# Program order for the loads of the transposed weight sections of a two-layer hybrid encoder

## The chip, the cores and the metric

The kernel runs on one core of one Trainium2 chip. The metric is the device time of one execution in microseconds (us); of several runs the median counts. A profile is one more execution, taken by the hardware profiler; its times are counted from the start of its span. The engines are called PE (TensorE, matmuls), PEld (its weight loads), DVE (VectorE), ACT (ScalarE), POOL (GpSimd) and SP (SyncE, which here issues every DMA).

## The reference

Two layers, each `x <- x + W_out(concat[A(h) * silu(g_A), B(h) * silu(g_B)])` with `h = RMSNorm(x)`, on 2048 tokens of width 1024, and a last RMSNorm. All inputs and the output are float32.

```python
def hybrid_layer(x, norm_gain, w_in, w_out, rel_bias, cos, sin):
    hn = rms_norm(x, norm_gain)
    proj = hn @ w_in                      # 1024 x 4096
    aq, ak, av, ag, rq, rk, rv, rg = jnp.split(proj, cuts, axis=-1)
    ya = chunked_rel_attention(aq, ak, av, rel_bias)   # 8 heads x 64, own chunk + 8 before
    yr = chunkwise_retention(rq, rk, rv, cos, sin)     # 4 heads x 128, recurrent over chunks
    y = jnp.concatenate([ya * silu(ag), yr * silu(rg)], axis=-1)
    return x + y @ w_out
```

A is a softmax attention with a learned bias by distance; B is a retention with decay, rotary phases and an RMS norm for each head.

## The kernel before, in words

Every float32 operand of a dense product is split into an upper and a lower half in float16, and three products of halves are summed, so a 128x512 result of depth 1024 takes 24 matmuls.

**Tiling.** A layer's heads are worked in four groups s = 0 to 3 (two attention heads and one retention head each), and a group's 2048 tokens in four blocks n = 0 to 3 of 512. A stage is named (layer, group, block). In each stage `dense_T` (L620) computes q, k of the attention and q, k of the retention, transposed (results `dT`, matmuls at L746), and `dense_V` (L753) the values and gates (`dV`, L766). One stage later `attention` (L792) and `retention` (L881) work on the block, between the dense matmuls.

**Rounds.** `run` (L1158) draws the work in rounds: eight dense matmuls (a third of a result), then what is due of the delayed steps (`tick`), a list's entry, a step of the attention, the entry's second half, and one or more steps of the background work (`pull`). dense_T and dense_V have twelve rounds each. The attention of a block has 24 rounds: every third issues the scores of one unit (128 tokens of one head, eight units in a block), and the product with v (`o`, L836 and L837) of a unit is issued some six rounds later. Between them lie DVE (bias and maximum, L818), ACT (exponential and upper half, L821 and L823), POOL (lower half, L824) and SP: one round after the scores, L826 transposes the probabilities of the unit by DMA (`pT<-pq`, up to 128x1280 elements of float16).

**Weight sections.** A group's weights come in sections of 1024x128 floats (512 KB): four for dense_T (`stT`, class `Sections`, L359) and four for dense_V (`stV`, `prep_V`, L434). `load_sec` (L295, its DMA at L300) puts a section into a slot of the pool `w4`, which has three. ACT squares it (L317) with a row sum, DVE casts the sum (`mbT`, L324), PE adds over the partitions (`ms`, L331), DVE makes a power of two of it (L144 and the following lines), and ACT and DVE split the section into its halves (L338, L341). Then the slot is free. `prep_T` (L402) does this for the next group's dense_T in 25 steps of background work, started in the round 0 of (l, s, 1): step 1 loads section 0, step 2 section 1, step 3 squares section 0, step 8 loads section 2, step 9 squares section 1, step 14 loads section 3, steps 15 and 21 square sections 2 and 3. The first round takes two steps, the later ones one.

**Group 1 of layer 0** is prepared by a list written out by hand (L1476 and the following lines). It has one entry for each of the first 96 rounds, from round 0 = the first of dense_V of (0,0,0), to which `weight_steps` (L1208) adds the names: `Tin0` to `Tin3` load the dense_T sections, `Tsq0` to `Tsq3` square them, `Uin0` and so on do the same for dense_V. In the same rounds the names `xin`, `xsq`, `xhi`, `xlo`, `xdma` load, normalise, split and transpose the last blocks of x, the tokens' tiles 12 to 15 going through the same slots of `w4`, and `v` is a step of the rotary tables.

**The order of the work.** PE, ACT, DVE and POOL execute in the order in which the program is traced. SP's queue does not: the compiler's scheduler fills it by its own estimate of when each DMA's inputs and slot are there, so a load whose slot is free can stand far ahead of its place in the program. Slots of a pool go to tiles in the order in which these are made. `in_turn` (L589) is the exception: it calls `tc.keep_in_program_order`, by which an instruction may not be queued ahead of the SP instruction traced just before it. Already in turn are the stores of y (L852, L926), the copies of q (L654), the rotary tables (L629, L630), a group's first bias tile (L576) and section 2 of each dense_V (L434). Each queue's instructions are issued in order, and SP waits at the head of its queue.

Of the kernel before, what the change touches and what calls it, by code (L numbers as in the profile page):

```python
# [18 lines left out]
P = 128  # L19
# [8 lines left out]
def hybrid_trunk(ctx: ExitStack, tc: tile.TileContext, x, pos, gain, gcol, w_in, w_out, rel, fgain,  # L28
# [6 lines left out]
    NS = SEQ // 512  # L35
# [259 lines left out]
    def load_sec(src, nm, halves=False, turn=False):  # L295

        v = src.rearrange("(k p) c -> p k c", p=P)
        if not halves:
            st = w4.tile([P, KT, P], F32, tag="w4", name=f"st{nm}")
            i = sp.dma_start(st, v)  # L300
            if turn:
                in_turn(i)
            return [(st, 0, KT)]
        h = KT // 2
        st = [b2.tile([P, 3 - i, 512], F16, tag=("rot2", "rot3")[i], name=f"st{nm}_{i}") for i in range(2)]
        st = [t_[:, 0:2].rearrange("p a c -> p (a c)").bitcast(F32).rearrange("p (k c) -> p k c", c=P) for t_ in st]
        for i in range(2):
            sp.dma_start(st[i], v[:, i * h:(i + 1) * h, :])
        return [(st[i], i * h, (i + 1) * h) for i in range(2)]
# [49 lines left out]
    class Sections:  # L359
# [15 lines left out]

        def load(self, j):
            o = TSEC[j] * 512 + self.s * P
            self.sts.append(load_sec(w_in[self.l, :, o:o + P], f"{self.nm}{j}", self.halves))

        def squares(self, j):  # L380
            nm = f"{self.nm}{j}"
# [177 lines left out]
    def bias_scratch(l, s):  # L559
        for hh in range(2):  # L560
            h = 2 * s + hh
            d = dp.tile([P * RELW], F32, tag=f"toep{h % 4}", name=f"toep{l}_{h}")
            i = sp.dma_start(d.rearrange("(p w) -> p w", w=RELW),
                             rel_d[l * 8 + h:l * 8 + h + 1, 1:RELW + 1].to_broadcast([P, RELW]))
            if (l, s) != (0, 0):
                tc.keep_in_program_order(i)
            toep[l, h] = d
        yield

    def bias_tiles(l, s, g):  # L570

        g.bias = []
        for hh in range(2):
            h = 2 * s + hh
            bt = b3.tile([P, 640], F32, tag="bias", name=f"bias{l}_{h}")
            i = sp.dma_start(bt, toep[l, h][127:127 + P * (RELW - 1)].rearrange("(p w) -> p w", w=RELW - 1)[:, 0:640])  # L576
            if hh == 0:
                in_turn(i)
            yield
            pool.memset(bt[64:128, 0:64], NEG)  # L580
            pool.memset(bt[0:64, 576:640], NEG)
            act.activation(bt, bt, AF.Copy, scale=g.ci[:, 0:1])
            g.bias.append(bt)
            yield
# [4 lines left out]
    def in_turn(i):  # L589

        if not ring.get("free"):
            return
        tc.keep_in_program_order(i)
# [9 lines left out]
    def later(k, fn):  # L603
        deferred.append([k, fn])
# [529 lines left out]
    def push(gen, steps):  # L1134
        bg.append([gen, steps])
# [11 lines left out]
    def drain(gen):  # L1147
        for _ in gen:
            pass
# [3 lines left out]
    def grp(l, s):  # L1153
        if (l, s) not in groups:
            groups[l, s] = Grp()
        return groups[l, s]
# [184 lines left out]
    def go_on(*gens):  # L1341
        for g_ in gens:
            next(g_, None)
# [123 lines left out]
    def do(names):  # L1467
        for nm in names.split():
# [24 lines left out]
    LAYER = [("", "yl0 yl1"), ("ys1", ""), ("", "xl0"), ("ys0", "yc0"), ("", "yh0"), ("", "yc1"), ("", ""),  # L1493
# [31 lines left out]
    for l in range(DEPTH):  # L1525
        gO = [Grp(), Grp()]
        go = Grp()
        for s in range(NSW):
            g = grp(l, s)
            for n in range(NS):  # L1530
                first = (l, s, n) == (0, 0, 0)
                if not first:
                    st = St()
                    states[l, s, n] = st
                    dT = dense_T(l, s, n, g, st)
                else:
                    st = st0
                if n == 0 and not first:
                    bs, bt = bias_scratch(l, s), bias_tiles(l, s, g)
                    later(3, lambda bs=bs: next(bs))  # L1540
                    for k in (7, 11, 17, 21):
                        later(k, lambda bt=bt: next(bt))
                if (l, s) == (0, 0) and 0 < n < NS - 1:
                    pairs = [xs0[0], w4.tile([P, D], F32, tag="w4", name="rows8") if n == 1 else xs0[1]]
                    pairs = [(w_[:, 0:D], w_[:, D:2 * D]) for w_ in (r_.bitcast(F16) for r_ in pairs)]
                    norm_steps(range(4 * n + 4, 4 * n + 8), late[0:4] if n == 1 else None, pairs)
                    if n == 2:
                        t3 = tables((3,), [xs0[3][:, i * 256:(i + 1) * 256] for i in range(4)])
                        steps["v"] = lambda: go_on(t3)
                if (l, s, n) == (0, 1, 2):  # L1550
                    for l_ in range(1, DEPTH):
                        gr = gain_scale(l_)
                        later(2, lambda gr=gr: next(gr))
                        later(10, lambda gr=gr: next(gr))
                        later(18, lambda gr=gr: next(gr))
                if (l, s, n) == (0, 0, NS - 1):
                    weight_steps()
                elif n == 1 and (l, s) != (0, 0):
                    if s + 1 < NSW:
                        push(prep_T(l, s + 1, grp(l, s + 1)), 25)  # L1560
                    else:
                        push(prep_O(l, gO[0], go), 9)
                if n == NS - 1 and s == 1 and l + 1 < DEPTH:
                    gain_load(l + 1)
                if n == 2 and 0 < s < 3:
                    push(prep_Omax(l, go, 4 * s - 4, 4 * s), 13 if s == 1 else 16)
                last = n == NS - 1 and s == NSW - 1
                if last:
                    us = []
                    sections = layer_steps(l, go, gO, us)  # L1570
                    ring["listed"] = iter(LAYER if l + 1 < DEPTH else LAST)
                if not first:
                    run(dT, att, 12 if last else 10 if n == 0 else 18 if (l, s, n) == (0, 0, NS - 1) else 22 if (l, s) == (0, 0) else 24)
                if n == NS - 1 and (l, s) != (0, 0):
                    if s + 1 < NSW:
                        push(prep_V(l, s + 1, grp(l, s + 1)), 23)
                run(dense_V(l, s, n, g, st), att, 24 if n == NS - 1 and s < NSW - 1 else 12)
                if first:
                    sp_order.__exit__(None, None, None)
                    ring["free"] = True  # L1580
                if att[0] is not None:
                    drain(att[0])
                att = [attention(l, s, n, g, st, states.get((l, s, n - 1)))]
        pull(1000)
        if l + 1 == DEPTH:
            ring["fg"] = b3.tile([P, D], F32, tag="wh", name="fg")
            sp.dma_start(ring["fg"], fgain.to_broadcast([P, D]))
        wT = sections() if l + 1 < DEPTH else None
        wo = wout(l, go, gO, us, wT)

        def rounds_of(k):
            run((next(wo) for _ in range(k)), att, k)

        rounds_of(6 * NT - 6)
        run(wo, att, 15)
# [60 lines left out]
```

## Time and profile before

| | |
|---|---|
| three runs | 2003.07, 2003.18, 2006.47 us |
| median | 2003.18 us |
| the profiled execution's own time | 2003.99 us |
| its span, first to last instruction | 2002.2 us |
| PE busy | 1976.9 us |
| DVE, ACT, POOL busy | 1231.6, 1155.0, 700.2 us |
| DMA engines busy with queue 1 | 68.1% of 16 engines' span |
| loads of `stT` at L300 | 27, of which 24 belong to groups 1 to 3 |

A row of the timeline reads: start, duration, engine and line, operation, out<-in, and in brackets how long the engine sat idle before it and what ended that. SPq is SP's queue; the duration of its row is that of the issue, not of the transfer. A row of waits reads: who waited, for whom, the sum in us, how often, the longest. In rows of groups the three figures of a duration are minimum, median and maximum in ns, and the last line of such a view gives the time from a DMA's issue to its landing in us. A busy time of PE has the modelled ends of its matmuls in it, which overlap.

### The profile page before, as it was taken

The page shows a single profiled execution, that of the slowest core. Times are in us where ns is not written, and L with a number is a line of the kernel's source. Part 1 is how long each engine was busy: PE and PEld are TensorE (multiplying, and loading weights), DVE is VectorE, ACT ScalarE, POOL GpSimd, SP SyncE. Part 2 cuts the span into 40 slices and gives each one's busy share as a digit, 9 for nine tenths or more (in the row PEclk, how much of TensorE's full clock was granted, in tenths as well). Part 3 has the DMA queues.
Part 4 walks back from the last instruction along what each step waited for, and adds up shares of the span by engine and source line. Part 5 has one row for each costly group of instructions (what it writes and reads, how often), then busy time and mean ns, then how long its engine had stood idle before and what let it go on. Part 6 is the DMA issues. An engine that isn't in the chain of part 4 may idle for free.

```text
span 2002.2 us, 36754 instructions
## 1 busy us (share of the span) xinstructions
PE 1976.9 (99%) x12894; PEld 1041.2 (52%) x12894; DVE 1231.6 (62%) x3664; ACT 1155.0 (58%) x2522; POOL 700.2 (35%) x701
## 2 busy tenths in 40 slices
PE   7999999999999999999999999999999999999998
PEld 5455555555555555554444555555555555555544
DVE  8787756665656655677544556555655565557544
ACT  8667756565656645656345556565656565456432
POOL 1444333434444334420013444344343443343100
PEclk9999999999999999999999999999999999999999
DMA  8899756576556655899974457564756575558864
GB/s 253 194 189 191 168 118 135 134 156 136 126 133 143 143 121 116 197 235 275 241 175 99 102 114 169 120 148 104 173 120 148 106 179 125 122 121 194 234 200 137
DMA packets 651706, 315.05 MB, mean 157 GB/s; under 512 B 465248, under 2 KB 608096, under 8 KB 651520
## 3 DMA queue, kind: packets, MB, share of 16 engines
q1 hardware_dynamic: 651520, 312.70, 68.1%
q8 instruction: 101, 1.65, 0.4%
q14 instruction: 85, 0.70, 0.1%
HBM read 123.26 MB, written 41.98 MB: 83 GB/s over the span
## 4 chain that ended last, share of the span: by engine, by line
PE 92%; DMA 3%; ACT 1%; SPq 1%; DVE 1%; issue 1%; POOL 1%; POOLq 0%; ACTq 0%; DVEq 0%
PE dV L766 31%; PE dT L746 30%; PE dO L1114 16%; PE r L871 4%; PE o L836 3%; PE S L814 3%; PE S L815 3%; PE o L837 2%; DMA pT<-pq 1%; DMA hTh<-in_x_dram 0%; SPq L1400 0%; DMA stT<-in_w_in_dram 0%; DMA yly<-hTh 0%; DMA hTl<-in_x_dram 0%; SPq L543 0%
## 5 line engine op out<-in xcount | busy, mean ns | idle before, releaser
L824 POOL TENSOR_TENSOR pq<-sc,pq 128x640 f16<-128x640 f32 (+4 forms) x256 | 322.5, 1260 | 957.4 <-ACT pq L823 482.5
L821 ACT ACTIVATE sc<-sc,mq,cT 128x640 f32<-128x640 f32 (+4 forms) x256 | 218.4, 853 | 403.9 <-DVE mq L820 291.9
L766 PE MATMUL dV<-whV,hTh 128*128 128x512 f16 x1024 | 351.5, 379 | 0.0
L766 PE MATMUL dV<-wlV,hTh 128*128 128x512 f16 x1024 | 351.5, 379 | 0.0
L766 PE MATMUL dV<-whV,hTl 128*128 128x512 f16 x1024 | 351.5, 379 | 0.0
L746 PE MATMUL dT<-hTh,whT 128*128 128x512 f16 x1008 | 346.6, 379 | 0.7 <-PE dV L766 0.7
L746 PE MATMUL dT<-hTh,wlT 128*128 128x512 f16 x1008 | 346.6, 379 | 0.0
L746 PE MATMUL dT<-hTl,whT 128*128 128x512 f16 x1008 | 346.6, 379 | 0.0
L766 PEld LDWEIGHTS <-hTh 128*128 128x128 f16 x2048 | 196.0, 98 | 211.6 <-DVE gt L784 0.4
L746 PEld LDWEIGHTS <-whT 128*128 128x128 f16 x2016 | 192.1, 98 | 206.0 <-issue 1.1
L818 DVE CUSTOM_DVE_ANT_0 sc<-S,bias 128x640 f32<-128x640 f32 (+4 forms) x256 | 188.5, 736 | 140.7 <-PE S L815 139.9
L1114 PE MATMUL dO<-whO,yhy 128*128 128x512 f16 x504 | 191.0, 379 | 1.2 <-DMA yhy<-hTh 1.2
L1114 PE MATMUL dO<-whO,yly 128*128 128x512 f16 x504 | 191.0, 379 | 0.2 <-DMA yly<-hTh 0.2
L1114 PE MATMUL dO<-wlO,yhy 128*128 128x512 f16 x504 | 191.0, 379 | 0.0
L823 ACT ACTIVATE pq<-sc 128x640 f16<-128x640 f32 (+4 forms) x256 | 171.5, 670 | 8.1
L1114 PEld LDWEIGHTS <-yhy 128*128 128x128 f16 x1008 | 98.0, 98 | 114.5 <-DMA yhy<-hTh 1.4
L766 PEld LDWEIGHTS <-hTl 128*128 128x128 f16 x1024 | 99.0, 98 | 109.8
L746 PEld LDWEIGHTS <-wlT 128*128 128x128 f16 x1008 | 97.4, 98 | 108.3 <-DVE wlT L1437 0.3
L814 PE MATMUL S<-k,q 128*128 128x128 f16 (+3 forms) x592 | 142.4, 267 | 0.0
L836 PE MATMUL o<-v,pT 128*128 128x129 f16 x1120 | 132.4, 221 | 3.1 <-DMA pT<-pq 3.0
L815 PE MATMUL S<-k,q 128*128 128x128 f16 (+3 forms) x592 | 129.3, 266 | 0.0
L837 PE MATMUL o<-v,pT 128*128 128x65 f16 x1120 | 125.7, 193 | 0.0
(359 smaller groups left out, 3245.0 us busy)
## 6 DMA issues: line engine op xcount, KB each, us to landing
q<-qq SPq DMA_DIRECT2D x128, 128.0 KB, 2.4
yyy<-y_d SPq DMA_DIRECT2D x32, 512.0 KB, 4.6
stT<-in_w_in_dram SPq DMA_DIRECT2D x27, 512.0 KB, 5.1
stV<-in_w_in_dram SPq DMA_DIRECT2D x26, 512.0 KB, 4.7
k<-kk SPq DMA_DIRECT2D x128, 64.0 KB, 2.0
swp<-rot SPq DMA_DIRECT2D x64, 128.0 KB, 3.0
tabc<-tab SPq DMA_DIRECT2D x32, 256.0 KB, 2.9
tabs<-tab SPq DMA_DIRECT2D x32, 256.0 KB, 3.0
```

The costliest lines, as they stand in the source:

```text
L746: pe.matmul(ps, w_[:, j, kt, :], h_[:, kt, :], start=(m == 0), stop=(m == 23))
L766: pe.matmul(ps, h_[:, kt, a * P:(a + 1) * P], w_[:, kt, :], start=(m == 0), stop=(m == 23))
L814: pe.matmul(o, st.q[:, hx, 0, cs], k_, start=True, stop=False)
L815: pe.matmul(o, st.q[:, hx, 1, cs], k_, start=False, stop=True)
L818: dve.tensor_tensor_reduce(out=v, in0=S[:, 0:w], in1=g.bias[hx][:, 640 - w:640], scale=1.0, scalar=-3.0e38, op0=ALU.add, op1=ALU.max, accu ...
L821: act.activation(v, v, AF.Exp, bias=m[:, 0:1], scale=g.c[:, 0:1])
L823: act.activation(pq[:, 0:w], v, AF.Copy)
L824: pool.tensor_tensor(pq[:, w:2 * w], v, pq[:, 0:w], op=ALU.subtract)
L836: pe.matmul(o[:, u.hx, 0:129], u.p[:, b, :], v_, start=(b == 0), stop=False)
L837: pe.matmul(o[:, u.hx, 0:65], u.p[:, u.nb + b, :], v_[:, 0:65], start=False, stop=(b == u.nb - 1))
L871: pe.matmul(out_, w_, m_, start=(i == 0), stop=(i + 1 == len(pairs)))
L1114: pe.matmul(ps, h_[:, kt, :], w_[:, kt, :], start=(m == 0), stop=(m == 23))
```

## The change

The loads of the dense_T sections get `in_turn` in every group but the first of each layer (`self.s > 0`). The list of the first 96 rounds is changed in the entries of three loads, and keeps its length: by count, `Tin0` moves from round 61 to round 50, `Tin1` from 61 to 55 and `Tin2` from 62 to 58, each to the end of its round; `Tin3` stays in round 67, the squares stay in rounds 62, 63, 64 and 71. Since the names are now used in stage (0,0,2), `weight_steps` is called there and no longer at (0,0,3).

```diff
         def load(self, j):
             o = TSEC[j] * 512 + self.s * P
-            self.sts.append(load_sec(w_in[self.l, :, o:o + P], f"{self.nm}{j}", self.halves))
+            self.sts.append(load_sec(w_in[self.l, :, o:o + P], f"{self.nm}{j}", self.halves, self.s > 0))
...
-                   ("xmul14 xrs15", ""), ("", "xdma12"), ("xhi14", "v"), ("", "xlo13"), ("", ""), ("", "v xmul15 v"),
-                   ("xdma13", ""), ("", "xhi15"), ("", "v xlo14"), ("v", ""), ("v xdma14 v", "v"), ("", "xlo15"),
-                   ("", ""), ("xdma15", ""), ("", ""), ("Tin0 Tin1", ""), ("Tsq0", "Tin2"), ("Tsq1", ""),
-                   ("Tsc1", "Tsq2 Tsc0"), ("", ""), ("Thi0", "Tlo0"), ("", "Tin3 Tsc2"), ("Thi1", "Thi2"), ("Tlo1", ""),
...
+                   ("xmul14 xrs15", ""), ("", "xdma12"), ("xhi14", "v"), ("", "xlo13"), ("", "Tin0"), ("", "v xmul15 v"),
+                   ("xdma13", ""), ("", "xhi15"), ("", "v xlo14"), ("v", "Tin1"), ("v xdma14 v", "v"), ("", "xlo15"),
+                   ("", "Tin2"), ("xdma15", ""), ("", ""), ("", ""), ("Tsq0", ""), ("Tsq1", ""), ("Tsc1", "Tsq2 Tsc0"),
+                   ("", ""), ("Thi0", "Tlo0"), ("", "Tin3 Tsc2"), ("Thi1", "Thi2"), ("Tlo1", ""), ("", "Uin0 Tlo2"),
...
-                if (l, s, n) == (0, 0, NS - 1):
+                if (l, s, n) == (0, 0, 2):
                     weight_steps()
-                elif n == 1 and (l, s) != (0, 0):
+                if n == 1 and (l, s) != (0, 0):
```

The lines of the diff that are left out hold the rest of the list, broken at other places but with the same entries.

8 rows, old and new, of the table steps are left out of this document.

## The prediction

> **What bounds the kernel.** I read the page first, then the waits of the matmul engine, then the stretches around the few waits that matter.
>
> ```profile
> span 2002.2 us, 36754 instructions
> PE 1976.9 (99%) x12894; PEld 1041.2 (52%) x12894; DVE 1231.6 (62%) x3664; ACT 1155.0 (58%) x2522; POOL 700.2 (35%) x701
> ```
>
> TensorE is busy for all but 25.3 us (2002.2 - 1976.9), most of it at the start. So a change of transfers can win only what TensorE now waits, and it costs nothing until TensorE waits more. The waits of PE from 50 us on:
>
> ```profile
> PE o L836 <- DMA pT<-pq: 3.0, 4, 1.2
> PE dO L1114 <- DMA yhy<-hTh: 1.2, 1, 1.2
> PE dT L746 <- PE dV L766: 0.7, 1, 0.7
> PE dO L1114 <- DMA yly<-hTh: 0.2, 1, 0.2
> ```
>
> That is 5.1 us behind the start of the kernel, and only the first row lies where weight sections are loaded. It is the product of the attention's probabilities with v (`o`, L836), waiting for the transposed probabilities `pT`. Its fourth time lies at the end of layer 0; the other three are these, from PE's timeline, the matmul before the wait and the one after it:
>
> ```profile
> 173.19 0.38 PE L746 MATMUL dT<-hTh,wlT 128*128 128x512 f16 x1
> 174.44 0.23 PE L836 MATMUL o<-v,pT 128*128 128x129 f16 x1 [0.88 <-DMA pT<-pq]
> ...
> 239.42 0.38 PE L746 MATMUL dT<-hTh,wlT 128*128 128x512 f16 x1
> 240.37 0.23 PE L836 MATMUL o<-v,pT 128*128 128x129 f16 x1 [0.57 <-DMA pT<-pq]
> ...
> 252.96 0.38 PE L766 MATMUL dV<-whV,hTh 128*128 128x512 f16 x1
> 253.17 0.38 PE L766 MATMUL dV<-whV,hTl 128*128 128x512 f16 x1
> 254.75 0.23 PE L836 MATMUL o<-v,pT 128*128 128x129 f16 x1 [1.20 <-DMA pT<-pq]
> ```
>
> Where nothing is late, a dense matmul starts 0.21 us after the one before (252.96 to 253.17), although its row says 0.38, since matmuls overlap. So the time lost is the step less 0.21: 1.04, 0.74 and 1.37 us, **3.15 us** in all. Now SP's queue just ahead of each:
>
> ```profile
> 167.53 0.57 SPq L300 DMA_DIRECT2D stT<-in_w_in_dram  x1
> 168.21 3.05 SPq L826 DMA_TRANSPOSE pT<-pq  x1
> ...
> 231.75 0.50 SPq L300 DMA_DIRECT2D stT<-in_w_in_dram  x1
> 233.30 3.72 SPq L826 DMA_TRANSPOSE pT<-pq  x1
> ...
> 245.73 1.12 SPq L300 DMA_DIRECT2D stT<-in_w_in_dram  x2
> 247.34 3.33 SPq L826 DMA_TRANSPOSE pT<-pq  x1
> ```
>
> Each late transpose stands directly behind a load of a weight section (`stT`, 512 KB; at 245.73 there are two). The chain that ended last runs through two of these transposes, from issue to landing:
>
> ```profile
> 168.21 6.19 DMA pT<-pq
> 247.34 7.37 DMA pT<-pq
> ```
>
> An undisturbed one of the same size, in the second such stage of layer 1, lands 3.0 us after its issue:
>
> ```profile
> DMA to landing us min/median/max: 3.0/3.0/3.0
> ```
>
> **The change, part by part.** It adds no work, removes none, and moves 24 loads of 512 KB: four for each of groups 1 to 3 of both layers. Each may no longer be queued ahead of the SP instruction traced just before it. ACT, DVE, POOL and PE keep the written order.
>
> *Group 1 of layer 0, the list.* The three early loads move in the list from the rounds 61, 61 and 62 to 50, 55 and 58, counted from dense_V of (0,0,0). Freely placed, the third stands at 167.53 in SP's queue. In the new list the SP instruction traced just before it is a pT transpose, of the same round's tick (a unit of the attention is issued every third round, its transpose a round later; rounds 55 and 58 are such rounds). Pinned, the load at 167.53 has to come behind the transpose at 168.21. That transpose then starts near 167.5 and lands, by the undisturbed 3.0, near 170.5, ahead of its use at 173.4 (173.19 + 0.21). The wait of 1.04 goes. The load itself starts near 169 and is read last of the three:
>
> ```profile
> L317 ACT ACTIVATE whT<-stT x3: 1040/1052/1057, 172.5 to 178.4; 128x1024 f16<-128x1024 f32 x3
> ...
> DMA to landing us min/median/max: 3.2/5.1/10.9
> ```
>
> With the median of all `stT` landings, 5.1, it is there at 174.1, before 178.4; at the slowest, 10.9 (a row that includes the crowded start), it would be 1.5 us late. The two before it are read in rounds 62 and 63, twelve and eight rounds behind their places. A round is at least eight dense matmuls of 0.21, 1.7 us, so they have 13 us and more. The mask load and the tile objects are only created earlier.
>
> *Group 2 of layer 0.* Its loads at 231.75 and 245.73 now come with prep_T's steps, in the first round of dense_T(0,1,1), near 272.6. The transposes at 233.30 and 247.34 lose the neighbour: minus 0.74 and 1.37. What else loads the queue there (toep, the bias tile, swp) stays, and in later groups the same stage, with the same other loads, makes PE wait nowhere: the rows of waits above have no place left for it.
>
> *The new place.* In groups 2 and 3 of layer 0 and of layer 1 (four places) the first round of prep_T takes two steps, so two loads come together, behind the store of y traced before them (272.26), while ACT's square stands only one round on:
>
> ```profile
> 272.26 0.32 SPq L852 DMA_DIRECT2D y_d<-ya  x1
> 274.20 3.94 SPq L826 DMA_TRANSPOSE pT<-pq  x2
> 276.35 1.04 ACT L317 ACTIVATE whT<-stT 128x1024 f16<-128x1024 f32 x1
> 277.51 0.16 DVE L324 CAST mbT<-m1T 128x1 bf16<-128x1 f32 x1 [1.55 <-ACT whT L317]
> 278.64 0.60 ACT L644 ACTIVATE qq<-dT 128x512 f16<-128x512 f32 x1 [1.16 <-PE dT L746]
> 280.00 2.40 SPq L654 DMA_DIRECT2D q<-qq  x4
> 280.17 0.22 PE L836 MATMUL o<-v,pT 128*128 128x129 f16 x1
> 282.45 0.17 PE L331 MATMUL msT<-mbT,ones 128*128 128x1 bf16 x1
> ```
>
> SP is idle from 272.58 (272.26 + 0.32) to 274.20, so the pair fits in at 272.6 and 273.2. Two prices follow. First the square: the nearest pair in the trace is this one, with its landings and with the transpose behind it:
>
> ```profile
> 1437.07 1.21 SPq L300 DMA_DIRECT2D stT<-in_w_in_dram  x2
> 1440.02 1.71 SPq L826 DMA_TRANSPOSE pT<-pq  x1
> ...
> DMA to landing us min/median/max: 4.3/4.8/5.3
> DMA to landing us min/median/max: 4.2/4.2/4.2
> ```
>
> A first load landing 4.3 after issue is there at 276.9, with 5.1 at 277.7: ACT starts its square 0.6 to 1.4 us late. Behind it ACT sits idle for 1.16, so 0.2 at most is passed on, and PE needs the result (DVE's cast, 277.67) only at 282.45: 4.8 us of cover. Cost nothing. All four engines' work that queues behind the square has this cover; the tightest of it is that sum.
>
> Second, the transpose at 274.20 is now the one behind two loads. Its use is at 280.17, so it may take 6.0 us. By the pair of 1437.07 it lands 7.1 us after the first load's issue (1440.02 + 4.2 - 1437.07): 279.7, **no wait**. By the pair of 245.73 it lands 9.0 after (247.34 + 7.37 - 245.73): 281.6, a wait of **1.4**. Which is nearer?
>
> ```profile
> 245.00:255.00 10.00, 8.80 (x65) 4.72 (x63) 5.83 (x19) 6.40 (x16) 7.79 (x9) 1.00 1.16 224
> 272.00:281.00 9.00, 9.00 (x69) 4.99 (x68) 3.38 (x14) 4.63 (x13) 2.33 (x3) 1.00 0.22 51
> 1436.50:1445.00 8.50, 8.50 (x62) 4.68 (x61) 4.40 (x14) 5.56 (x11) 6.22 (x8) 1.00 0.97 232
> ```
>
> The last two columns are the DMA engines' share and GB/s. The new place is the quietest, 51 GB/s without the pair, and 1 MB over 9 us adds 117: well under the 224 of the bad case and the 232 of the good one. I take no wait in three places, and 0.5 us once, as an estimate: in the first such stage of layer 1 the same transpose already lands 4.8 after issue instead of 3.0:
>
> ```profile
> DMA to landing us min/median/max: 4.8/4.8/4.8
> ```
>
> Both ends, 0 and 5.6 (4 x 1.4), stay in the range. The Trainium skill, "DMA: Bandwidth & Descriptors", section "Queues, rings and completion order", says that each DMA engine takes its descriptors in ring order. That speaks against this change, since it puts the transpose behind the whole pair; the three waits above agree with it. By that rule alone, taken at the crowded pair's rate, the sum would be -3.15 + 5.6 = +2.4.
>
> The third and fourth loads come with steps 8 and 14, seven rounds before their squares, 12 us or more. No cost. In group 1 of layer 1 no attention runs ahead of the place, and the loads come early enough.
>
> **The sum:** -1.04 - 0.74 - 1.37 + 0.5 = -2.65, rounded -2.6. The profiled execution took 2003.99, 1.8 over its span and 0.8 over the median of 2003.18; the waits are differences, so I take them from the median: **2000.6 us**.
>
> **The rivals.**
> *The pair makes transposes late.* In all four places the wait is 1.4: +5.6 - 3.15, so 2005.6. For it: the three waits of today, all behind such loads. Against it: 51 GB/s, and the good pair.
> *The square comes late (slower).* If the scheduler places the pair behind the two transposes (274.20 + 3.94 = 278.14), the first load lands at 283.2 with 5.1; 1.32 (276.35 to 277.67) later the cast is done, 284.6, and PE's sum at 282.45 waits 2.1, four times: +8.4 - 3.15, 2008.5. Behind the four copies of q too (280.00 + 2.40) it is 288.8, 6.4 each, 2025. It decides from an issue of the first load at 276.0 (282.45 - 1.32 - 5.1). For it: the square follows one round after the load, and SP's place is chosen by estimates. Against it: SP stands idle there for 1.6 us, and the transpose waits for POOL until 274.2. In the Trainium skill, "TensorE: Matmul & The Clock Gate", the section on the array's architecture states that ScalarE and VectorE take instructions strictly in order. By that rule everything behind a late square is late, as this rival has it.
> *The change doesn't do what it says:* the waits stay, as toep, bias and swp cause them, or the loads fall before other transposes. Then -1 to 0: 2002.5.
> *More goes than counted:* the remaining waits at the layer's end (1.2 + 0.2, and the fourth of L836) move as the queue is ordered anew: another 2 us, 1998.6.
>
> **How the numbers follow.** Forecast 0.60, pair late 0.11, square late 0.11, waits stay 0.13, more goes 0.05. The range leaves out the late square (0.11), most of the last case and the end of the late pair: **1999.0 to 2005.7**. Within 0.2% (4.0 us) is about what a measurement of this kernel can tell from no change: from 1999.2 to 2007.2. Faster than that: 0.07 (more goes, and 0.02 of the forecast's edge). Slower: 0.13 (late square, and 0.02 of a late pair). Same: 0.80.
>
> **What would show it.** Right: no row "PE o <- DMA pT" near 174, 240 and 254 us; `stT` loads near 272.6, and in the same place of the three later stages, behind a store of y and ahead of the transpose; ACT's idle time before the square under 1.5 us; `pT` of those places landing before its use. Wrong: PE waiting for `ms` (L331) on a cast, or for `pT` some 8 us into those four stages; or the three waits still there with no load ahead of them.

## The result, and the profile after

| | before | after |
|---|---|---|
| median, 19 runs each | 2003.23 us | 2000.33 us |
| lowest and highest | 2000.75, 2006.47 us | 1999.04, 2001.41 us |
| the profiled execution's own time | 2003.99 us | 1999.99 us |

The changed kernel takes 2.90 us less, a ratio of 0.9984 with a 95% interval of 0.9977 to 0.9991. The forecast was 2000.6. The page of the changed kernel:

```profile
span 1998.2 us, 36745 instructions
PE 1976.6 (99%) x12894; PEld 1041.8 (52%) x12894; DVE 1229.8 (62%) x3664; ACT 1154.0 (58%) x2522; POOL 699.1 (35%) x701
```

PE's busy time is what it was (1976.6 after 1976.9); its idle time went from 25.3 to 21.6 us. All of PE's waits from 50 us on (who waited for whom, sum in us, how often, the longest):

```profile
PE o L836 <- DMA pT<-pq: 1.2, 2, 0.7
```

Four rows have become one, and its two times lie near 103 us and 890 us, where no load was moved. (The wait near 103 us has its row in the run with group 2 alone and in the one with an eighth of the bytes too, whose queue there is that of before; it differs from run to run.) The waits at 174, 240 and 255 us are gone. SP's queue ahead of each of the three places shows why, first around the transpose that stood directly behind the load at 167.53:

```profile
169.06 1.34 SPq L826 DMA_TRANSPOSE pT<-pq  x1
170.45 0.58 SPq L300 DMA_DIRECT2D stT<-in_w_in_dram  x1
```

The load stands behind the transpose now (170.45), and the issue of that transpose occupies the queue for 1.34 us instead of 3.05. Its view, and that of the later one of the next group, at 247.02 (the issue in ns, then the landing in us):

```profile
L826 SPq DMA_TRANSPOSE pT<-pq x1: 1337/1337/1337, 169.1 to 169.1; - x1
DMA to landing us min/median/max: 3.2/3.2/3.2
...
L826 SPq DMA_TRANSPOSE pT<-pq x1: 2461/2461/2461, 247.0 to 247.0; - x1
DMA to landing us min/median/max: 3.8/3.8/3.8
```

Before, these two took 6.19 and 7.37 from issue to landing. The one between them, at 232.98 now, lands after 4.5 instead of 7.0. The new place of group 2's first two loads, on SP, then ACT's square of the first, then PE's product with v and its sum over the partitions (`msT`):

```profile
261.94 0.38 SPq L374 DMA_DIRECT2D msk<-in_dmask_dram  x1
262.37 0.45 SPq L300 DMA_DIRECT2D stT<-in_w_in_dram  x1
264.56 2.38 SPq L826 DMA_TRANSPOSE pT<-pq  x1
...
269.63 0.58 SPq L300 DMA_DIRECT2D stT<-in_w_in_dram  x1
...
270.99 0.38 SPq L852 DMA_DIRECT2D y_d<-ya  x1
...
273.91 1.04 ACT L317 ACTIVATE whT<-stT 128x1024 f16<-128x1024 f32 x1
...
277.73 0.22 PE L836 MATMUL o<-v,pT 128*128 128x129 f16 x1
...
280.01 0.17 PE L331 MATMUL msT<-mbT,ones 128*128 128x1 bf16 x1
```

This is not the place of the prediction. The two loads aren't a pair: the first stands at 262.37, directly behind the load of the mask (L374), and the second 7.3 us later. The first lands at 269.3 by its view,

```profile
L300 SPq DMA_DIRECT2D stT<-in_w_in_dram x1: 454/454/454, 262.4 to 262.4; - x1
DMA to landing us min/median/max: 6.9/6.9/6.9
```

4.6 us ahead of the square, which has no idle time before it, as before the change. Neither PE row carries a bracket: nothing is late.

### The profile page after: what moved, and what is told of

It reads as the page before. It is cut to its first block, busy times and chain, and to the rows that moved or that the text cites. A ratio compares the mean times of both kernels' runs of the same rounds, so it can differ in the third digit from the quotient of the medians.

```text
span 1998.2 us, 36745 instructions
## 1 busy us (share of the span) xinstructions
PE 1976.6 (99%) x12894; PEld 1041.8 (52%) x12894; DVE 1229.8 (62%) x3664; ACT 1154.0 (58%) x2522; POOL 699.1 (35%) x701
## 4 chain that ended last, share of the span: by engine, by line
PE 55%; DVE 1%; DMA 0%; issue 0%; ACT 0%; POOLq 0%; POOL 0%; SPq 0%; ACTq 0%; DVEq 0%
PE dT L746 17%; PE dV L766 17%; PE dO L1114 14%; PE r L871 2%; PE o L836 2%; PE S L814 2%; PE S L815 2%; PE o L837 1%; DMA pT<-pq 0%; DMA x_d<-hTl 0%; PE ptn L1017 0%; DVE hTl L990 0%; DVE sc L818 0%; DVE hTl L1117 0%; DVE hTl L1012 0%
```

## The experiments

The theory: a load of 512 KB queued directly ahead of a transpose of the probabilities makes that transpose land late, and that is all that the change removes. Two rivals: the gain comes from the other 16 moved loads, or it is the order of the queue as such and not what the load brings. After the result there were two more questions: what the pair would have cost where the prediction had placed it, and what the new places are worth. The kernel before took 2003.37 (2001.03 to 2004.97, 33 runs) beside the first four experiments, and 2003.1 (2001.21 to 2004.64, 18 runs) beside the last three.

### Group 1 of layer 0 alone

The new list, and only that group's loads in turn.

```diff
-self.halves, self.s > 0))
+self.halves, (self.l, self.s) == (0, 1)))
```

The edit is to the changed kernel.

> Only the four loads of group 1 of layer 0 are pinned, with the new list; all other loads stand as before. Theory (a load directly ahead of a transpose of the probabilities makes that transpose land late, and PE waits for it): the wait at 174 us (1.04 lost) goes, since the third load now stands behind the transpose; those at 240 and 255 us (0.74 and 1.37) stay. 2003.2 - 1.0 = 2002.2 us. Rival (the gain comes from elsewhere, or the three waits are chance of a run): all three move or stay together, and the time is that of before or of after.

Measured: 2002.02 us (2001.01 to 2003.43, 11 runs), a ratio of 0.9995 (0.9986 to 1.0004). PE's waits for `pT` near the three places:

```profile
238.93 0.23 PE L836 MATMUL o<-v,pT 128*128 128x129 f16 x1 [0.22 <-DMA pT<-pq]
...
253.43 0.23 PE L836 MATMUL o<-v,pT 128*128 128x129 f16 x1 [1.33 <-DMA pT<-pq]
```

The first of the three waits has no row any more, the two of group 2 stay. By the medians that is 1.35 us, and 1.04 was counted for it. The interval reaches past no change, so the time alone would not show it. The rows do.

### Group 2 of layer 0 alone

The old list, and only that group's loads in turn.

```diff
-self.halves))
+self.halves, (self.l, self.s) == (0, 2)))
```

The edit is to the kernel before, as it is in the next two runs.

> Only the four loads of group 2 of layer 0 are pinned, with the old list. Theory: the waits at 240 and 255 us go (2.1 lost together), the one at 174 us stays; 2003.2 - 2.1 = 2001.1 us. Rival (the other loads of that stage, bias scratch, bias tile, tables and swaps, make the transposes late): both waits stay, 2003.2 us.

Measured: 2000.87 us (1999.97 to 2003.16, 11 runs), 0.9988 (0.9979 to 0.9997). The one wait left of the three:

```profile
174.42 0.23 PE L836 MATMUL o<-v,pT 128*128 128x129 f16 x1 [0.62 <-DMA pT<-pq]
```

That is the mirror of the run before: 240 and 255 us are clean, 174 us is not. 2.5 us by the medians against a count of 2.11.

### All the other groups, without these two

```diff
-self.halves))
+self.halves, self.s > 0 and (self.l, self.s) not in ((0, 1), (0, 2))))
```

The list is the old one.

> Only the loads of group 3 of layer 0 and of groups 1 to 3 of layer 1 are pinned, with the old list. Theory: no wait of PE stands beside any of these loads before, so nothing is won, and the new place has room, so nothing is lost: 2003.2 us, all three waits still there. Rival (the new place costs: the transpose behind the load late by up to 1.4 in three stages): up to 2007.4 us, with waits of PE for a transpose near 479, 1264 and 1468 us.

Measured: 2002.9 us (2001.84 to 2004.24, 11 runs), 1.0 (0.9992 to 1.0009).

```profile
174.56 0.23 PE L836 MATMUL o<-v,pT 128*128 128x129 f16 x1 [1.09 <-DMA pT<-pq]
...
240.43 0.23 PE L836 MATMUL o<-v,pT 128*128 128x129 f16 x1 [0.50 <-DMA pT<-pq]
...
254.88 0.23 PE L836 MATMUL o<-v,pT 128*128 128x129 f16 x1 [0.87 <-DMA pT<-pq]
```

All three waits are there (and a short fourth, 0.23 at 247.50), and PE has no wait at the new places of these loads (near 479, 1264 and 1468 us). The 16 loads of the four remaining groups, two thirds of what the change moves, win or lose nothing that these runs can tell (the interval leaves room for 1.6 us less and 1.8 more). The first rival falls. The three parts give 1.35, 2.5 and 0.5 us, 4.3 in sum where the whole gives 2.9; each has an uncertainty of nearly 2 us, so this is no contradiction and no proof that they add up.

### An eighth of the bytes in the old order

All loads as before, in the old order and with the old list. The four loads of group 2 bring 64 KB instead of 512 KB, in 128 rows of 512 bytes instead of 1024, and every later use of the section stays. The lines behind the edit are 3 higher.

```diff
+            if nm[:4] == "T0_2":
+                sp.dma_start(st[:, 0:1], v[:, 0:1])
+                return [(st[:, 0:1].to_broadcast([P, KT, P]), 0, KT)]
             i = sp.dma_start(st, v)
```

> SP's queue as in the kernel before, but the four loads of group 2 of layer 0 bring 64 KB in place of 512 KB: the first 128 rows of each section stand for all eight, so this leaves out seven eighths of that group's dense_T weights. Theory (the bytes in front of the transpose make it late): the waits at 240 and 255 us go as if the loads had been moved, the wait at 174 us stays; 2001.1 us. Rival (the order itself, or a fixed price of one more transfer ahead of a transpose): the waits stay, 2003.2 us.

Measured: 2001.05 us (2000.23 to 2002.13, 11 runs), 0.9988 (0.9979 to 0.9997). SP's queue, where the loads still stand directly ahead of the transposes:

```profile
231.57 0.43 SPq L301 DMA_DIRECT2D stT<-in_w_in_dram  x1
233.13 1.38 SPq L829 DMA_TRANSPOSE pT<-pq  x1
...
243.60 1.81 SPq L301 DMA_DIRECT2D stT<-in_w_in_dram  x2
...
247.17 1.99 SPq L829 DMA_TRANSPOSE pT<-pq  x1
```

The two transposes from issue to landing, and PE's waits for `pT` in the whole run:

```profile
DMA to landing us min/median/max: 4.5/4.5/4.5
DMA to landing us min/median/max: 3.4/3.4/3.4
...
PE o L839 <- DMA pT<-pq: 1.1, 2, 0.6
```

The issues of the transposes take 1.38 and 1.99 us instead of 3.72 and 3.33, and they land after 4.5 and 3.4 us instead of 7.0 and 7.37. The waits at 240 and 255 us are gone; the two that are left are at 174 us (0.61), where the load is whole, and near 102 us (0.53). It is what the load ahead brings, not the place: the second rival falls. The run changes bytes and rows alike, so it can't say which of the two counts. A load in flight beside a transpose isn't enough either: in the changed kernel the one at 170.45 is issued directly behind the transpose of 169.06, which lands after 3.2. The Trainium skill, "DMA: Bandwidth & Descriptors", section "Queues, rings and completion order", has each DMA engine take its descriptors in ring order; the run agrees, since in the same order an eighth of the bytes ahead makes neither transpose late for PE.

### The two loads where the prediction placed them

The changed kernel, with the load of the mask traced behind the loads 0 and 1, so that load 0 is pinned behind the store of y and not behind the mask.

```diff
-        w = Sections(l, s, g)
+        w = Sections(l, s, g, mask=False)
...
+            if j == 0:
+                w.mask(g, s)
```

> The changed kernel, but in the 25-step preparation the mask's load is traced behind the first two section loads, so the first of these is pinned behind the store of y, where the prediction had put it: in SP's queue it now stands directly ahead of the last transpose of the stage before, and the second load directly behind that transpose. Theory (a load directly ahead makes a transpose late by what it has not yet brought): that transpose, issued 0.4 us behind the load, lands between 5.9 and 6.9 us after the load's issue (the nearest pairs of before) and is used 6.3 us after it: a wait of 0 to 0.6 in each of three or four stages, 2000.3 to 2002.7 us, with transposes landing under 1 us before their use there. The square is late by 2 to 3 us and PE doesn't wait for its sum. Rival (a quiet place has room): landing as before, 2000.3 us.

Measured: 2000.95 us (1999.46 to 2001.84, 11 runs), 0.9988 (0.998 to 0.9997). The queue:

```profile
269.84 0.32 SPq L854 DMA_DIRECT2D y_d<-ya  x1
270.21 0.43 SPq L300 DMA_DIRECT2D stT<-in_w_in_dram  x1
271.78 2.21 SPq L828 DMA_TRANSPOSE pT<-pq  x1
274.04 0.57 SPq L300 DMA_DIRECT2D stT<-in_w_in_dram  x1
...
274.60 1.06 ACT L317 ACTIVATE whT<-stT 128x1024 f16<-128x1024 f32 x1 [0.58 <-DMA stT<-in_w_in_dram]
```

The first load stands where the prediction had it, behind the store of y; the scheduler put a transpose between it and the second. The square is 0.58 late, and PE's sum still isn't. The transpose lands 3.9 us after its issue, 2.1 ahead of its use; the tightest place is the same stage of layer 1, where the transpose behind the first load takes longest:

```profile
L828 SPq DMA_TRANSPOSE pT<-pq x1: 1997/1997/1997, 1257.3 to 1257.3; - x1
DMA to landing us min/median/max: 5.6/5.6/5.6
...
1263.28 0.22 PE L838 MATMUL o<-v,pT 128*128 128x129 f16 x1
```

It lands at 1262.9, 0.4 us ahead of its use. That is 7.2 us behind the load's issue, later than the 5.9 to 6.9 expected, but the use comes 7.5 behind that issue and not 6.3, so the expected wait of up to 0.6 doesn't come. There the square is 2.21 late, and PE's sum (1265.57) still doesn't wait. PE's four waits for `pT` in this run (2.2 us) stand near 103, 878, 890 and 1792 us. So even in the predicted place no wait arises, and the time can't be told from that of the changed kernel (2000.33). A transpose behind both loads at once did not come about here, so its price stays untested.

### The square made late

In the changed kernel, the loads 0 and 1 are traced in the round of the first square, which puts them behind the last transposes. The lines are 3 higher here too.

```diff
-        w = Sections(l, s, g)
-        w.load(0)
+        w = Sections(l, s, g, mask=False)
...
-            if j < 3:
+            if 0 < j < 3:
                 w.load(j + 1)
             yield
+            if j == 0:
+                w.load(0)
+                w.load(1)
+                w.mask(g, s)
```

> The changed kernel, but the first two section loads of the 25-step preparation are traced two steps later, in the round of the first square, behind the first transpose of the new stage. Theory (ACT and DVE wait in order at the square and the cast of its sum, and PE at the sum over partitions): the load is issued 3.8 us later than the square's place, lands 5.1 after that, and PE waits some 2 us for the sum in each of five stages: 2000.3 + 10 = 2010 us, with waits of PE at L331 for the cast. Rival (the slack of the three engines hides it): 2000.3 us.

Measured: 2015.97 us (2014.64 to 2018.07, 5 runs), 1.0068 (1.0056 to 1.0081). SP, ACT and PE in the first of the five stages, and PE's waits from 50 us on:

```profile
275.00 1.20 SPq L300 DMA_DIRECT2D stT<-in_w_in_dram  x2
...
279.71 1.06 ACT L317 ACTIVATE whT<-stT 128x1024 f16<-128x1024 f32 x1 [6.47 <-DMA stT<-in_w_in_dram]
...
279.04 0.38 PE L749 MATMUL dT<-hTh,whT 128*128 128x512 f16 x1
281.11 0.16 PE L331 MATMUL msT<-mbT,ones 128*128 128x1 bf16 x1 [1.68 <-DVE mbT L324]
```

```profile
PE msT L331 <- DVE mbT L324: 9.0, 7, 2.0
PE o L839 <- DMA pT<-pq: 4.1, 5, 1.2
PE dT L749 <- DMA hTl<-hTl: 0.5, 1, 0.5
```

PE would have read the sum at 279.25 (279.04 + 0.21) and does so at 281.11, 1.86 late. The prediction's rule for this rival, issue plus 5.1 plus 1.32, gives 281.4. Five such squares make up 8.6 of the 9.0 us. The time is 6 us above the 2010 expected, and part of that is the old mechanism: of the 4.1 us, three waits (0.93, 0.63 and 0.56) stand behind a transpose that has a third load directly ahead. SP's rows of the first, and the product that waits:

```profile
290.99 0.43 SPq L300 DMA_DIRECT2D stT<-in_w_in_dram  x1
291.53 1.20 SPq L829 DMA_TRANSPOSE pT<-pq  x1
...
297.68 0.23 PE L839 MATMUL o<-v,pT 128*128 128x129 f16 x1 [0.93 <-DMA pT<-pq]
```

The transpose lands at 297.6, 6.1 after its issue. The other two of the five waits stand behind none of the moved loads: 1.22 at 1805 us, where a load of W_out (`stO`) is queued directly ahead of the transpose, and 0.80 at 544 us, where the nearest load ahead was issued 4.3 us before the transpose. The loss over the changed kernel is 15.6 us by the medians, 14.6 by the spans. The rows give 12.4 (9.0 + 4.1 + 0.5 - 1.2), and a wait costs the step 0.16 more than its bracket (1.04 against 0.88 in the first wait of before), 1.8 for the eleven waits more: 14.2.

The changed kernel has the same neighbours there:

```profile
287.58 0.43 SPq L300 DMA_DIRECT2D stT<-in_w_in_dram  x1
288.12 1.21 SPq L826 DMA_TRANSPOSE pT<-pq  x1
```

That transpose lands at 293.3, 5.2 after its issue, and is used at 295.5. So a load ahead of a transpose is not a loss in itself; there are 2.2 us of cover. In the kernel with the late square PE would have taken the transpose 5.2 us after its issue (297.68 - 0.93 - 291.53) and not 7.4 (295.5 - 288.1), so the cover is used up.

### All loads in turn, with the old list

The edit is to the kernel before; its list stays, with `("Tin0 Tin1", "")` in round 61 and `("Tsq0", "Tin2")` in round 62.

```diff
-self.halves))
+self.halves, self.s > 0))
```

> All loads pinned as in the changed kernel, but with the list of before, where the first three loads of group 1 of layer 0 stand in the round before the first square and in its own. Theory: the three loads are queued together behind a transpose near 174.7 us, the second lands some 6 us later, and PE waits for its sum (round 64, near 175) until about 182: plus 7 to 9 us, 2007 to 2009 us. Rival (the list's move does nothing but remove the wait at 174 us): 2000.3 to 2001.3 us.

Measured: 2008.29 us (2007.9 to 2009.23, 8 runs), 1.0029 (1.0018 to 1.0039). SP, ACT and PE:

```profile
174.25 2.79 SPq L300 DMA_DIRECT2D stT<-in_w_in_dram  x3
...
179.20 1.06 ACT L317 ACTIVATE whT<-stT 128x1024 f16<-128x1024 f32 x1 [6.30 <-issue]
...
176.15 0.38 PE L746 MATMUL dT<-hTh,whT 128*128 128x512 f16 x1
182.34 0.19 PE L331 MATMUL msT<-mbT,ones 128*128 128x1 bf16 x2 [5.81 <-DVE mbT L324]
...
182.78 0.63 PE L746 MATMUL dT<-hTl,whT 128*128 128x512 f16 x1
183.20 0.63 PE L746 MATMUL dT<-hTh,whT 128*128 128x512 f16 x1
```

The three loads go out together at 174.25; in the list the first two stand one round ahead of the first square, the third in its round. The square starts at 179.20, when the first load has landed, and PE stands still for 5.81 us. Pinned loads need the other places in the list: the run with group 1 alone, which has them, came out 1.35 us ahead by its medians, within the scatter; without them, all loads pinned take 8.0 us more than the changed kernel (2008.29 - 2000.33).

## Why the prediction was right, and which step of it was wrong

- **What bounds the kernel, and the three waits:** right. Each goes when the loads ahead of it are moved (groups 1 and 2 alone) and stays when only the others are (all the others alone). In all nine profiles the wait at 174 us is there exactly where the third load stands directly ahead of that transpose (before, group 2 alone, the others alone, an eighth of the bytes), and those at 240 and 255 us exactly where group 2's loads do so whole (before, group 1 alone, the others alone). Their count of 3.15 us stands against 2.90 for the whole, where the interval of the ratio makes it 1.8 to 4.6 us.
- **Group 1, the list:** right. The transpose was put near 167.5 with a landing 3.0 later; it is at 169.06 and lands 3.2 later. The third load was to start near 169 and to be there at 174.1 for a square at 178.4. It starts at 170.45 and lands 4.9 later, at 175.4; its square starts at 178.50.
- **Group 2, the transposes lose their neighbour:** right, with a smaller benefit for each than an undisturbed landing of 3.0 would give (4.5 and 3.8). It is enough.
- **The new place:** wrong. The prediction set the pair near 272.6, "behind the store of y traced before them (272.26)". It is in fact 262.37 and 269.63. The step that failed is the reading of what is traced just before load 0. `prep_T` makes its `Sections` first, whose `__init__` traces the load of the mask (L374). The mask is not in turn, so the scheduler takes it early, and load 0, pinned behind the mask and behind nothing else, follows it there. With the mask traced later, load 0 does stand behind the store of y. Why the second load comes 7.3 us behind the first, no run shows.
- **The price of the pair, "0.5 us once":** it did not arise, first because there is no pair. At the predicted place there is no wait either, with 0.4 us to spare in the tightest stage. Without the 0.5 the sum is -3.15, or 2000.0 us; that the forecast of 2000.6 with it lies as near to the measured 2000.33 is luck, since the interval of 1.8 to 4.6 can't tell the two apart.
- **The third and fourth loads, "No cost":** right, but not for the reason given. Their squares have time enough; what decides is that the transpose behind the third, 5.2 instead of 3.0 from issue to landing, still has 2.2 us of cover.
- **The late square:** rightly left out of the forecast, with a right price. It was priced at 2.1 us a stage for a load issued behind the transposes, and made so it costs 1.86 in the first stage. The prediction counted four such places and there are five (group 1 of layer 1 is prepared by the same steps), and it left out that PE's wait also shifts what follows, where three transposes behind a third load then came late for 2.1 us more. So its 2008.5 stands against a measured 2015.97.
- **"More goes than counted":** the profiled execution after has less waiting at the end of layer 0 (0.45 us) than that of before (1.2 + 0.2 and 0.37 of the 3.0). But the end of layer 0 holds none of the moved loads, and the waits there are 0.6 us with group 1 alone, 1.0 with an eighth of the bytes, and none with group 2 alone or the others alone. So these are differences from run to run, and the medians hold none of it that can be told.

What stays open: whether the three parts add up to the whole within a microsecond, which runs that scatter by 2 to 4 us can't say, what a transpose directly behind two loads costs in the quiet stage, and whether it is the bytes or the rows of a load that count.

## What to carry to other kernels

In this kernel a transfer that an engine waits for came late where a load of 512 KB was queued directly ahead of it, though its own issue began only 0.7 to 1.6 us behind that of the load: look at what is queued directly ahead of the late one, and move it to where the transfer behind it has cover. Pinning an instruction to its place in the program says only what it may not pass, namely the one traced just before it, so find that very instruction and ask whether it is itself free to float. And a pinned load needs a place ahead of its reader by its full landing, since the scheduler no longer makes up for a late place.

## What the runs showed of the hardware

The price of PE's long wait was more than the wait. Where the three loads went out together, the granted clock was halved behind it (the columns are the stretch, its length, busy time and instructions of PE, PEld, DVE, ACT and POOL, then PE's clock, the DMA engines' share and GB/s):

```profile
182.30:185.00 2.70, 2.65 (x9) 1.00 (x9) 2.49 (x12) 1.59 (x3) 0.00 (x0) 0.50 0.55 134
```

For some 5.4 us, up to 187.8, a dense matmul starts 0.42 us after the one before (182.78 to 183.20) and not 0.21, which is another 2.7 us: together with a wait of 5.98 (182.34 - 176.15, less 0.21) it is 8.7, and the spans of the two kernels differ by 8.3. The waits of up to 2.0 us in the kernel with the late square left the clock at 1.00, here behind the first (1.68); behind the longest (2.00), from 1069.38 to 1072.00, it is 1.00 too:

```profile
281.10:284.00 2.90, 2.90 (x19) 1.53 (x19) 2.49 (x10) 1.22 (x4) 0.00 (x0) 1.00 0.25 56
```

The Trainium skill, "TensorE: Matmul & The Clock Gate", section "Part 1: The HAM clock gate (the "warmup" mystery)", gives half the clock after an idle window of about 3.4 us; both rows (0.50 behind a wait of 5.8 us, 1.00 behind one of 1.7) agree. The waits that this change is about, of 1.4 us and less, carry no such price: behind the longest, from 254.70 to 257.00 in the profile before, the clock is 1.00.
